# A two-layer decoder trunk on one core: two classes of scales instead of three in the feed-forward output products, part of their exponents on GpSimd, and other places for totals and weight squares

## The chip, the cores and the metric

The kernel runs on one core of a Trainium2 chip. The metric is device time in microseconds (us), the median over several executions. The engines are TensorE (PE in the profile), VectorE (DVE), ScalarE (ACT), GpSimd (POOL) and SyncE (SP), which issues the DMAs.

## The reference, cut to what matters

```python
D_MODEL, SEQ, DEPTH = 1024, 1024, 2
D_FF = 2816                                  # ceil(8 * 1024 / 3 / 256) * 256
...
def swiglu_ffn(x, w_in, w_out):
    gu = jnp.einsum("bsd,df->bsf", x, w_in)
    h = jax.nn.silu(gu[..., :D_FF]) * gu[..., D_FF:]
    return jnp.einsum("bsf,fd->bsd", h, w_out)

def reference(x, ...):
    h = x
    for layer in range(DEPTH):
        hn = rms_norm(h, mix_norm[layer])
        if layer % 2 == 0:
            mixed = rg_lru_block(hn, ...)
        else:
            mixed = stick_breaking_attention(hn, ...)
        h = h + mixed
        h = h + swiglu_ffn(rms_norm(h, ffn_norm[layer]), ffn_w_in[layer], ffn_w_out[layer])
    return rms_norm(h, final_norm)
```

All inputs and the output are f32. The change touches only the feed-forward part, which runs twice, once in each layer, with the same code.

## The kernel before, in words

**Products.** The matrix products of the feed-forward part are computed in a fast form for 2x2 blocks, with 7 products instead of 8. The seven products of a step are numbered k = 0 to 6 in the order in which PE does them. The weights of a product are sums and differences of quarters of the weight matrix: the tiles a, b, c and d (in the profile `wa`, `wb`, `wc`, `wd`). Each factor is held as two f16 tiles, a high part and a low part, so a product takes three matmuls, high by high (L155), high by low (L156) and low by high (L157). The high parts of weights are cut on ACT (L770), the low parts on DVE (L775), which subtracts the high part from the scaled f32 tile. DVE also makes the sums of quarters (L784 to L793).

**Scales.** f16 needs operands of a bounded size. So each tile is multiplied by a power of two before it is cut, and its product by the inverse afterwards. The power comes from a sum of squares: ACT squares a tile and adds up its rows (L753 for the weights of the first product, L1291 for the gated activations U, L1514 for the weights of the second), DVE adds the columns to a `part` of 128x1, PE adds over the partitions by a matmul of one column (L251, into `n_ps`), and a run of small DVE operations shifts exponent bits. A `Measure` does this for the weights of the first product in as many jobs: squares, `total` (L894), and `factors` (the matmul L251 and L244 to L248).

**Steps.** A layer's feed-forward part has steps f = 1 to 21 and then visits v = 0 to 12. Step f forms one of 22 column tiles of gate and up, multiplies silu(gate) by up (L1097 to L1103) into U, and stores operands of the second product, made from pairs of tiles, in DRAM (L1111 to L1127). Visit v multiplies some pairs p0 to p1 of such operands by the output weights and adds the results to the residual h (L1458 to L1464). In layer 0 f1 begins at 342 us, f12 at 547, f20 at 692, f21 at 711, v0 at 732, v2 at 757 and v9 at 884; layer 1 does the same about 1132 us later. Even steps from f4 to f18 also hold the matmuls `i_ps` into 128x256.

**The table of visits** is what the classes of scales cut through:

```python
VISITS = (
    (0, 0, 2), (1, 0, 3), (2, 0, 4), (3, 0, 4), (0, 2, 5), (1, 3, 7), (2, 4, 8),
    (3, 4, 8), (0, 5, 9), (1, 7, 11), (2, 8, 11), (3, 8, 11), (0, 9, 11),
)                                            # (rows d, first pair, end of pairs)
```

Pairs 0 to 3, 4 to 9 and 10 have each a power of their own. A visit over one class has one segment in `Weights`, and each cut of a weight tile is one instruction; a visit over two classes has two segments, and L770 and L775 issue two instructions for each tile, over parts of its columns. Such are v4 and v5 (pairs 3 and 4 in one visit) and v9 to v12 (pairs 9 and 10).

**Order.** PE, ACT, DVE and POOL run in an order that is written by hand: each step calls its pieces product by product, and `plan[kind, x, k]` holds the extra jobs that are put in at product k of step x. `add_up(g)` adds the columns of class g, `scales(g)` does its `n_ps` matmul and the exponents; they stand at (f8: k4, k6), (f20: k4, k6) and (v2: k4, k5). `measure` puts the jobs of each `Measure` into places. `spots` lists the places of the 44 squares L1514 of the output weights in each layer; the DMA that loads such a tile (L1511, 256 KB, on SP) is issued one step earlier at the same k. SP's order is chosen by a scheduler. The seven products share PSUM banks, so some products can begin only after ACT or DVE has read an earlier product out (L1079 and L1083 read products of gate to `G`, L1087 and L1092 those of up to `U`, L1458 those of a visit to `ta`, `tb`, `held` or `G`).

## Time and profile before

| | |
|---|---|
| median of 3 runs | 2097.0 us (2095.85 to 2099.33) |
| profiled execution | 2096.64 us, its span 2094.5 us, granted clock of PE 0.999 |
| PE busy | 2042.5 us, 98% of the span |
| DVE busy | 1853.6 us, 88% |
| ACT busy | 1437.9 us, 69% |
| POOL busy | 104.4 us, 5% |
| DMA | 331.8 MB, 158 GB/s over the span |

The span is one execution seen by the hardware profiler. A row of a timeline has the start, the duration, the engine, the line, the operation, the tiles written and read, and in brackets how long the engine stood idle before it and what released it. Matmuls are pipelined: a row of PE says 0.38 us, and the next begins 0.22 us after it. So PE's busy time runs past the moment at which PE could take the next matmul, and an idle time in brackets is shorter than what was lost by some 0.16 us.

### The profile page before, as it was taken

To read this page: it belongs to the slowest core of one execution; us is meant where nothing else is said; L and a number is where in the kernel's file an instruction comes from. 1 tells how busy PE (TensorE), PEld (TensorE's weight loads), DVE (VectorE), ACT (ScalarE), POOL (GpSimd) and SP (SyncE) were. 2 spreads that over 40 slices of the span, in tenths; PEclk is the share of its full clock that TensorE was granted. 3 is DMA by queue.
4 is the path that set the end of the run, shared out by engine and by line. 5 is a ranking of instruction groups with operands and counts; after the bars stand their busy time and mean duration, and the time that the engine had idled before them with its cause. 6 is when DMAs were issued, how large, how long until landed. Compare 5 with 4: busy or idle time off the path is not lost.

```text
span 2094.5 us, 28835 instructions
## 1 busy us (share of the span) xinstructions
PE 2042.5 (98%) x10058; PEld 1240.3 (59%) x10058; DVE 1853.6 (88%) x2878; ACT 1437.9 (69%) x2369; POOL 104.4 (5%) x114
## 2 busy tenths in 40 slices
PE   8999999999999999989999999999999999999998
PEld 7888885455545444438777777677445555434444
DVE  7887898989999889896999999977899999999887
ACT  6677447777777646566787888744867777765566
POOL 1000010000000000000011111202000000000002
PEclk9999999999999999999999999999999999999999
DMA  7231562644555655134888888972455456764412
GB/s 253 67 94 51 181 206 66 211 156 157 176 186 191 235 192 162 50 111 98 165 176 176 177 177 175 251 230 92 125 168 171 151 186 197 242 225 138 139 41 91
DMA packets 455217, 331.76 MB, mean 158 GB/s; under 512 B 167192, under 2 KB 362912, under 8 KB 455072
## 3 DMA queue, kind: packets, MB, share of 16 engines
q1 hardware_dynamic: 454912, 329.67, 54.6%
q8 instruction: 78, 1.28, 0.3%
q14 instruction: 67, 0.55, 0.1%
q10 hardware_dynamic: 160, 0.27, 0.0%
HBM read 208.74 MB, written 75.50 MB: 136 GB/s over the span
## 4 chain that ended last, share of the span: by engine, by line
PE 71%; DVE 19%; ACT 6%; issue 3%; DMA 1%; SPq 0%; DVEq 0%; ACTq 0%
PE p_ps L157 10%; PE p_ps L155 10%; PE p_ps L156 10%; PE qk_ps L155 4%; PE qk_ps L157 4%; PE qk_ps L156 4%; PE av_ps L2163 3%; PE a_ps L156 3%; PE a_ps L157 3%; PE a_ps L155 3%; PE ob_ps L155 3%; PE ob_ps L156 3%; PE ob_ps L157 3%; DVE v L1366 2%; DVE wa L775 2%
## 5 line engine op out<-in xcount | busy, mean ns | idle before, releaser
L157 PE MATMUL p_ps<-v,wb 128*128 128x512 f16 x524 | 199.5, 381 | 10.5 <-DVE wb L775 10.3
L155 PE MATMUL p_ps<-v,wb 128*128 128x512 f16 x524 | 199.0, 380 | 5.5 <-ACT G L1079 2.4
L157 PE MATMUL p_ps<-v,wc 128*128 128x512 f16 x524 | 198.6, 379 | 2.4 <-DVE wc L775 2.4
L156 PE MATMUL p_ps<-v,wb 128*128 128x512 f16 x524 | 199.3, 380 | 0.0
L155 PE MATMUL p_ps<-v,wc 128*128 128x512 f16 x524 | 198.6, 379 | 0.0
L156 PE MATMUL p_ps<-v,wc 128*128 128x512 f16 x524 | 198.6, 379 | 0.0
L157 PE MATMUL p_ps<-v,wa 128*128 128x512 f16 x396 | 150.1, 379 | 0.0
L156 PE MATMUL p_ps<-v,wa 128*128 128x512 f16 x396 | 150.1, 379 | 0.0
L155 PE MATMUL p_ps<-v,wa 128*128 128x512 f16 x396 | 150.0, 379 | 0.0
L770 ACT ACTIVATE wb<-sb,fac 128x1024 f16<-128x1024 f32 x44 | 50.5, 1148 | 105.4 <-DVE sb L790 105.4
L155 PE MATMUL qk_ps<-rh,whi 128*128 128x512 f32 x264 | 113.0, 428 | 0.0
L2089 ACT ACTIVATE w<-z_ps,rs 128x512 f32<-128x512 f32 (+2 forms) x168 | 96.8, 580 | 16.3 <-PE z_ps L2052 13.1
L155 PE MATMUL p_ps<-v,wd 128*128 128x512 f16 x254 | 96.2, 379 | 11.1 <-ACT G L1458 4.9
L2111 ACT CAST wx<-w 128x512 f16<-128x512 f32 (+1 forms) x140 | 80.1, 572 | 37.4 <-DVE w L2096 19.7
L156 PE MATMUL qk_ps<-rl,whi 128*128 128x512 f32 x264 | 103.5, 392 | 0.0
L157 PE MATMUL qk_ps<-rh,wlo 128*128 128x512 f32 x264 | 103.5, 392 | 0.0
L2096 DVE TENSOR_TENSOR_SCAN w<-w,unit 128x128 f32<-128x128 f32 (+1 forms) x112 | 93.5, 835 | 9.5 <-ACT w L2089 8.3
L157 PEld LDWEIGHTS <-wb 128*128 128x128 f16 x524 | 51.3, 98 | 80.7 <-DVE wb L775 22.6
L1366 DVE SCALAR_TENSOR_TENSOR v<-raw,gx,v 128x512 f16<-128x512 f32 x128 | 91.1, 745 | 7.8 <-ACT v L1365 7.6
L157 PE MATMUL p_ps<-v,wd 128*128 128x512 f16 x254 | 96.3, 379 | 1.5 <-DVE wd L775 1.5
L155 PE MATMUL a_ps<-xh,whi 128*128 128x512 f32 x248 | 97.0, 391 | 0.0
L156 PE MATMUL a_ps<-xl,whi 128*128 128x512 f32 x248 | 96.6, 390 | 0.1
(474 smaller groups left out, 5735.7 us busy)
## 6 DMA issues: line engine op xcount, KB each, us to landing
raw<-in_ffn_w_in SPq DMA_DIRECT2D x80, 512.0 KB, 4.3
raw<-in_ffn_w_out SPq DMA_DIRECT2D x144, 256.0 KB, 3.4
raw<-pd SPq DMA_DIRECT2D x128, 256.0 KB, 3.9
pd<-U SPq DMA_DIRECT2D x90, 256.0 KB, 2.3
raw<-in_attn_w_qkv SPq DMA_DIRECT2D x24, 512.0 KB, 4.3
raw<-in_lru_w_out SPq DMA_DIRECT2D x16, 512.0 KB, 3.5
h<-hd SPq DMA_DIRECT2D x32, 256.0 KB, 5.3
hd<-h SPq DMA_DIRECT2D x32, 256.0 KB, 3.7
```

The lines of the kernel that those rows point to most:

```text
L155: nc.tensor.matmul(ps, lhsT=wh, rhs=mh, start=first, stop=False, **kw)
L156: nc.tensor.matmul(ps, lhsT=wh, rhs=ml, start=False, stop=False, **kw)
L157: nc.tensor.matmul(ps, lhsT=wl, rhs=mh, start=False, stop=last, **kw)
L770: nc.scalar.activation(h, r, AF.Copy, scale=up)
L775: V.scalar_tensor_tensor(l, r, up, h, op0=ALU.mult, op1=ALU.subtract)
L1366: V.scalar_tensor_tensor(lo, raw, power_of(p), hi, op0=ALU.mult, op1=ALU.subtract)
L2089: nc.scalar.activation(F, ps[:, 0:n], AF.Sigmoid, scale=rs[:, j : j + 1])
L2096: nc.vector.tensor_tensor_scan(rev, rev, unit[:, NB - n :][:, ::-1], 0.0, op0=ALU.mult, op1=ALU.add)
L2111: nc.scalar.copy(wx[:, 0:m, 0], F)
L2163: nc.tensor.matmul(ps[:, c0:c1].rearrange("p (j c) -> p j c", c=P), lhsT=VV[q][:, hx, kb], rhs=t, start=first and i == 0, stop=last and i ...
```

## The change

The pairs are put into two classes, 0 to 3 and 4 to 10, instead of three. `segs` and `undo` follow, so v9 to v12 have one segment and v4 and v5 still two. `add_up` and `scales` are called with 0 (class 0), 3 (the output weights) and 1 (class 1) instead of 0, 1 and 2, at (f8: k4, k6), (f20: k4, k6) and (v2: k5, k6). At f20 only the exponent of the output weights is then worked out; that of the second class comes at v2. Some of the small operations (`inverses`, the sums of exponents, two of the `field`s) go to POOL. In `measure`, the squares, total and factors of the `Measure` of f20 move from k0, k1, k1, k2 to k0, k2, k2, k3, and the totals of the pair steps from k6 to k0 of the next step. `spots` is (x, k) for x = 4 to 18 and k = 0, 1, 3 instead of x = 2 to 19 with k = 0, 1 in even and 1, 3, 6 in odd steps; 44 places in both.

```diff
@@ -1267,22 +1267,19 @@
                         nc.sync.dma_start(dst, view[par])
                     return raw
 
-                groups = [int(p >= 4) + int(p >= 10) for p in range(p0, p1)]
-                g, m0 = groups[0], groups.count(groups[0])
-                cols_ = ((3,), (3,))[0] if m0 == m else (4, 5) if g == 0 else (6, 7)
-                segs = [(0, m0, gx[:, cols_[0] : cols_[0] + 1])]
-                if m0 < m:
-                    segs.append((m0, m, gx[:, cols_[1] : cols_[1] + 1]))
+                if p0 < 4 < p1:
+                    segs = [(0, 4 - p0, gx[:, 4:5]), (4 - p0, m, gx[:, 5:6])]
+                else:
+                    segs = [(0, m, gx[:, 3:4])]
                 return Weights(load, m, segs)
 
             def undo(u):
                 _, p0, p1 = VISITS[u]
-                i = 0 if p1 <= 4 else 2 if p0 < 4 else 1 if p1 <= 10 else 3
+                i = 0 if p1 <= 4 else 1 if p0 >= 4 else 2
                 return rx_[:, 4 + i : 5 + i], sums[1][:, i : i + 1]
 
-            power_of = lambda p: gx[:, int(p >= 4) + int(p >= 10) :][:, 0:1]
-            H = rx_.bitcast(I32)
-            G32 = gx.bitcast(I32)
+            power_of = lambda p: gx[:, int(p >= 4) :][:, 0:1]
+            G32, R32 = gx.bitcast(I32), rx_.bitcast(I32)
             tmp = wsq[0][:, 6:8]
             tmpi = tmp.bitcast(I32)
             psq = lambda f: (ymax[:, f : f + 1] if f < 2 * ND else wsq[0][:, f - 2 * ND : f - 2 * ND + 1])
@@ -1290,56 +1287,46 @@
             def square_u(f):
                 nc.scalar.activation(GT[f % 2][:, NB:].bitcast(BF16), UT[f % 3], AF.Square, accum_out=psq(f))
 
-            def add_up(g):
+            def add_up(what):
                 p = part16[0]
                 with nc.allow_low_precision(reason="a bound alone"):
-                    if g == 0:
+                    if what == 0:
                         V.tensor_reduce(p[:, 2:3], ymax[:, 0:8], axis=AX, op=ALU.add)
-                    elif g == 1:
+                    elif what == 3:
+                        V.tensor_reduce(p[:, 2:3], wosq[:, 0 : 2 * NF], axis=AX, op=ALU.add)
+                    else:
                         V.tensor_reduce(tmp[:, 0:1], ymax[:, 8:16], axis=AX, op=ALU.add)
-                        V.tensor_reduce(tmp[:, 1:2], wsq[0][:, 0:4], axis=AX, op=ALU.add)
+                        V.tensor_reduce(tmp[:, 1:2], wsq[0][:, 0:6], axis=AX, op=ALU.add)
                         V.tensor_add(p[:, 2:3], tmp[:, 0:1], tmp[:, 1:2])
-                        V.tensor_reduce(p[:, 3:4], wosq[:, 0 : 2 * NF], axis=AX, op=ALU.add)
-                    else:
-                        V.tensor_add(p[:, 2:3], wsq[0][:, 4:5], wsq[0][:, 5:6])
 
             def field(dst, src, a, b):
-                V.tensor_scalar(dst, src, float(a * EXP), float(b) * EXP, op0=ALU.mult, op1=ALU.add)
-
-            def exponent(at, ps):
-                V.tensor_scalar(tmp[:, 0:1], ps, 1e-30, 1.0, op0=ALU.max, op1=ALU.mult)
-                V.tensor_single_scalar(H[:, at : at + 1], tmpi[:, 0:1], 24, op=ALU.logical_shift_right)
-
-            def both_of(a, at, i):
-                x, y = H[:, a : a + 1], H[:, a + 1 : a + 2]
-                t0, t1 = tmpi[:, 0:1], tmpi[:, 1:2]
-                V.tensor_max(t0, x, y)
-                V.tensor_add(t0, t0, H[:, 3:4])
-                for k, z in enumerate((x, y)):
-                    V.tensor_sub(t1, z, t0)
-                    V.tensor_scalar(t1, t1, -202.0, 203.0, op0=ALU.max, op1=ALU.add)
-                    V.tensor_scalar(G32[:, at + k : at + k + 1], t1, float(EXP), 0.0, op0=ALU.mult, op1=ALU.add)
-                inverse(t0, i)
-
-            def inverse(q, i):
-                field(H[:, 4 + i : 5 + i], q, 1, -25)
-                V.tensor_scalar_mul(sums[1][:, i : i + 1], rx_[:, 4 + i : 5 + i], -1.0)
-
-            def scales(g):
+                eng = nc.vector if dst.shape[-1] == 1 and a < 0 else nc.gpsimd
+                eng.tensor_scalar(dst, src, float(a * EXP), float(b) * EXP, op0=ALU.mult, op1=ALU.add)
+
+            def inverses(q, i, n):
+                field(R32[:, 4 + i : 4 + i + n], q, 1, -25)
+                nc.gpsimd.tensor_scalar_mul(sums[1][:, i : i + n], rx_[:, 4 + i : 4 + i + n], -1.0)
+
+            def scales(what):
                 ps = pp.tile([P, NB], F32, tag="p", name="n_ps")
-                n = 2 if g == 1 else 1
-                over_partitions(ps[:, 0:n], part16[0][:, 2 : 2 + n])
-                exponent(g, ps[:, 0:1])
-                field(G32[:, g : g + 1], H[:, g : g + 1], -1, 203)
-                if g == 1:
-                    exponent(3, ps[:, 1:2])
-                    field(G32[:, 3:4], H[:, 3:4], -1, 203)
-                    for x in range(2):
-                        V.tensor_add(tmpi[:, 0:1], H[:, x : x + 1], H[:, 3:4])
-                        inverse(tmpi[:, 0:1], x)
-                    both_of(0, 4, 2)
-                elif g == 2:
-                    both_of(1, 6, 3)
+                over_partitions(ps[:, 0:1], part16[0][:, 2:3])
+                V.tensor_scalar(tmp[:, 0:1], ps[:, 0:1], 1e-30, 1.0, op0=ALU.max, op1=ALU.mult)
+                V.tensor_single_scalar(tmpi[:, 1:2], tmpi[:, 0:1], 24, op=ALU.logical_shift_right)
+                field(G32[:, what : what + 1], tmpi[:, 1:2], -1, 203)
+                V.tensor_copy(rx_[:, what : what + 1], tmpi[:, 1:2])
+                e0, e1, ew = (rx_[:, x : x + 1] for x in (0, 1, 3))
+                q = sums[0][:, 4:6]
+                if what == 3:
+                    nc.gpsimd.tensor_add(q[:, 0:1], e0, ew)
+                    inverses(q[:, 0:1], 0, 1)
+                elif what == 1:
+                    d = sums[0][:, 6:8]
+                    V.tensor_max(q[:, 1:2], e0, e1)
+                    nc.gpsimd.tensor_add(q[:, 1:2], q[:, 1:2], ew)
+                    nc.gpsimd.tensor_scalar(d, rx_[:, 0:2], q[:, 1:2], -202.0, op0=ALU.subtract, op1=ALU.max)
+                    nc.gpsimd.tensor_scalar(G32[:, 4:6], d, float(EXP), 203.0 * EXP, op0=ALU.mult, op1=ALU.add)
+                    nc.gpsimd.tensor_add(q[:, 0:1], e1, ew)
+                    inverses(q, 1, 2)
 
 
 
@@ -1478,7 +1465,7 @@
                 if (x, k) == (1, 0):
                     m, at = m2, ((1, 0),)
                 elif (x, k) == (NF - 2, 0):
-                    m, at = Measure(nw), ((x, 0), (x, 1), (x, 1), (x, 2))
+                    m, at = Measure(nw), ((x, 0), (x, 2), (x, 2), (x, 3))
                 elif (x, k) == (1, 3):
                     m, at = Measure(ahead), ((1, 3), (1, 4), (1, 5), (2, 0))
                 elif (x, k) == (NF - 4, 4):
@@ -1487,7 +1474,7 @@
                     m, at = Measure(ahead, early[3]), ((2, 0), (2, 1), (2, 4), (2, 5), (2, 6), (3, 2))
                 elif k == 3 and x + 2 in PAIRS and x > 2:
                     m = Measure(ahead, early[x + 1])
-                    at = ((x, 3), (x, 4), (x, 5), (x, 6), (x, 6), (x + 1, 2))
+                    at = ((x, 3), (x, 4), (x, 5), (x, 6), (x + 1, 0), (x + 1, 2))
                 else:
                     m, at = None, ()
                 for i, when in enumerate(at):
@@ -1500,11 +1487,11 @@
             early, squares_of = {}, []
             plan["f", 8, 4] = [lambda: add_up(0)]
             plan["f", 8, 6] = [lambda: scales(0)]
-            plan["f", 20, 4] = [lambda: add_up(1)]
-            plan["f", 20, 6] = [lambda: scales(1)]
-            plan["v", 2, 4] = [lambda: add_up(2)]
-            plan["v", 2, 5] = [lambda: scales(2)]
-            spots = [(x, k) for x in range(2, 20) for k in ((1, 3, 6) if x % 2 else (0, 1))][: 2 * NF]
+            plan["f", 20, 4] = [lambda: add_up(3)]
+            plan["f", 20, 6] = [lambda: scales(3)]
+            plan["v", 2, 5] = [lambda: add_up(1)]
+            plan["v", 2, 6] = [lambda: scales(1)]
+            spots = [(x, k) for x in range(4, 19) for k in (0, 1, 3)][: 2 * NF]
 
             def weigh_out(i):
                 t = loose(v)
```

What this does to the order of the instructions is seen at three places. The first is DVE at the end of f20 and the start of f21 in layer 0. Before, the last seven of 22 small operations of `scales(1)` stand ahead of the gate's product with `ob` (L1097) and the low part of tile b of f21 (L775):

```order
L1319 TENSOR_TENSOR wsq_91<-rx,wsq_91 128x1
L1320 TENSOR_SCALAR wsq_91<-wsq_91 128x1
L1321 TENSOR_SCALAR gx<-wsq_91 128x1
L1307 TENSOR_SCALAR rx<-wsq_91 128x1
L1326 TENSOR_SCALAR sums_94<-rx 128x1
L1097 TENSOR_TENSOR G_2727<-ob,G_2727 128x1024
L775 SCALAR_TENSOR_TENSOR wb<-sb,fac_98,wb 128x1024
```

In the changed program, DVE has there:

```order
L1353 SCALAR_TENSOR_TENSOR rbc_84<-acc_1969,gx,rbc_84 128x512
L1313 TENSOR_SCALAR wsq_91<-n_ps 128x1
L1314 TENSOR_SCALAR wsq_91<-wsq_91 128x1
L1304 TENSOR_SCALAR gx<-wsq_91 128x1
L1316 CAST rx<-wsq_91 128x1
L1097 TENSOR_TENSOR G_2727<-ob,G_2727 128x1024
L775 SCALAR_TENSOR_TENSOR wb<-sb,fac_98,wb 128x1024
```

Here are all the DVE operations of `scales(3)`: four between the low part of an operand of the visits (L1353, which was L1366) and L1097. The names `wsq`, `gx`, `rx` and `sums` are small tiles of exponents and scales.

The second place is ACT from the end of f11 to the middle of f12 in layer 0. `G_2727` and `U_2729` are the gate and up tiles, `wosq` the column of a square of output weights. Before:

```order
L770 ACTIVATE wb<-sb,fac_98 128x1024
L1291 ACTIVATE G_2727,ymax<-U_2731 128x1024
L1092 COPY U_2729<-p_ps 128x512
L1514 ACTIVATE junk,wosq<-raw_1_4262 128x512
L770 ACTIVATE wc<-raw,fac_98 128x1024
L1079 COPY G_2727<-p_ps 128x512
L1514 ACTIVATE junk,wosq<-raw_1_4282 128x512
L1099 ACTIVATE G_2728<-G_2728,fac_97 128x1024
```

After the change (the lines have other numbers: L1291 is L1288, L1514 is L1501):

```order
L770 ACTIVATE wb<-sb,fac_98 128x1024
L1288 ACTIVATE G_2727,ymax<-U_2731 128x1024
L1092 COPY U_2729<-p_ps 128x512
L770 ACTIVATE wc<-raw,fac_98 128x1024
L1079 COPY G_2727<-p_ps 128x512
L1501 ACTIVATE junk,wosq<-raw_1_4277 128x512
L1099 ACTIVATE G_2728<-G_2728,fac_97 128x1024
```

One square, that of f11's k6, has gone from between the reading of a product (L1092) and the high part of tile c (L770); it stood two rows ahead of the reading of f12's first product (L1079). The third place is DVE around v2's products k4 to k6 in layer 0; `part` is what the matmul into `n_ps` reads, `G`, `U` and `tb` are operands of pairs, `s` and `sb` sums of weight quarters, `g` the residual. Before:

```order
L790 TENSOR_TENSOR sb<-raw 128x512
L1304 TENSOR_TENSOR part_95<-wsq_91 128x1
L1124 TENSOR_TENSOR G_2728<-U_2729,tb 128x512
L1464 SCALAR_TENSOR_TENSOR g_2_1_6025<-p_ps,sums_94,g_2_1_6025 128x512
L793 TENSOR_TENSOR s_6676<-sb,raw 128x512
L1310 TENSOR_SCALAR wsq_91<-n_ps 128x1
L1311 TENSOR_SCALAR rx<-wsq_91 128x1
L1307 TENSOR_SCALAR gx<-rx 128x1
L1316 TENSOR_TENSOR wsq_91<-rx 128x1
L1317 ISA wsq_91<-wsq_91,rx 128x2
L1319 TENSOR_TENSOR wsq_91<-rx,wsq_91 128x1
```

After:

```order
L1451 SCALAR_TENSOR_TENSOR g_2_1_6026<-p_ps,sums_94,g_2_1_6026 128x512
L793 TENSOR_TENSOR s_6659<-sb,raw 128x512
L1298 TENSOR_REDUCE wsq_91<-ymax 128x1
L1299 TENSOR_REDUCE wsq_91<-wsq_91 128x1
L1300 TENSOR_TENSOR part_95<-wsq_91 128x1
L1127 TENSOR_TENSOR U_2731<-U_2729,U_2731 128x512
L1451 SCALAR_TENSOR_TENSOR g_6_0_6033<-p_ps,rx,g_6_0_6033 128x512
L1313 TENSOR_SCALAR wsq_91<-n_ps 128x1
L1314 TENSOR_SCALAR wsq_91<-wsq_91 128x1
L1304 TENSOR_SCALAR gx<-wsq_91 128x1
L1316 CAST rx<-wsq_91 128x1
L1324 TENSOR_TENSOR sums_93<-rx 128x1
```

The adding up to `part` is now three operations and stands behind L793 instead of ahead of L1124, and the exponents are four DVE operations (L1313 to L1316) and one for the pair of classes (L1324) instead of thirteen.

## Prediction

> **What bounds the kernel now.** I read the page's busy times and its chain first, then PE's waits, then each wait in the timelines of PE, ACT and DVE.
>
> ```profile
> PE 2042.5 (98%) x10058; PEld 1240.3 (59%) x10058; DVE 1853.6 (88%) x2878; ACT 1437.9 (69%) x2369; POOL 104.4 (5%) x114
> PE 71%; DVE 19%; ACT 6%; issue 3%; DMA 1%; SPq 0%; DVEq 0%; ACTq 0%
> ```
>
> PE sets the time, and the change takes no matmul away. So it can gain only what PE now loses in waits, at the places that it touches. DVE, at 88%, is the engine that makes most of these waits: it carries 19% of the chain. The waits of PE in the whole run (total, times, longest) name the causes:
>
> ```profile
> PE p_ps L157 <- DVE wb L775: 10.3, 11, 2.3
> PE p_ps L155 <- ACT G L1079: 2.4, 9, 0.3
> ```
>
> How much one wait costs is read from PE's timeline at f21 in layer 0:
>
> ```profile
> 716.08 0.38 PE L155 MATMUL p_ps<-v,wb 128*128 128x512 f16 x1
> 716.30 0.38 PE L156 MATMUL p_ps<-v,wb 128*128 128x512 f16 x1
> 718.93 0.39 PE L157 MATMUL p_ps<-v,wb 128*128 128x512 f16 x1 [2.26 <-DVE wb L775]
> ```
>
> Matmuls start 0.22 us apart, though a row says 0.38. The third should have started at 716.52 and started at 718.93: 2.41 us lost where the bracket says 2.26. So each bracket costs 0.15 us more than it says; I add that below.
>
> **The change part by part.**
>
> *The burst of exponents at f20 (`scales(1)`).* DVE's timeline shows the first and the last of its 22 small operations, and what they hold up:
>
> ```profile
> 713.05 0.15 DVE L1310 TENSOR_SCALAR wsq<-n_ps 128x1 f32<-128x1 f32 x1
> 716.40 0.15 DVE L1326 TENSOR_SCALAR sums<-rx 128x1 f32<-128x1 f32 x1
> 716.47 1.22 DVE L1097 TENSOR_TENSOR G<-ob,G 128x1024 f32<-128x1024 f32 x1
> 717.60 1.28 DVE L775 SCALAR_TENSOR_TENSOR wb<-sb,fac,wb 128x1024 f16<-128x1024 f32 x1
> ```
>
> From 713.05 to 716.47 is 3.42 us, 0.155 for each. The change leaves four, 0.62 us, so the gate and `wb` come 2.8 us earlier. `wb`, done at 718.88, would be done at 716.08, which is 0.44 before PE wants it at 716.52. PE comes earlier by what f20 gains (below), but so does DVE, whose wait of 1.23 for the same square ends with it. The whole 2.41 goes, in both layers alike: 4.8. In layer 1 something follows the wait. These are a window right behind it in layer 1, one behind the same wait in layer 0 (length; busy of PE, weight loads, DVE, ACT, POOL; granted clock, DMA share, GB/s), and the wait in layer 1:
>
> ```profile
> 1850.80:1854.20 3.40, 3.40 (x10) 1.17 (x9) 2.46 (x3) 0.00 (x0) 0.00 (x0) 0.51 0.37 108
> 717.90:721.10 3.20, 2.17 (x10) 0.99 (x11) 3.20 (x4) 0.97 (x1) 0.00 (x0) 1.00 0.00 0
> 1850.39 0.39 PE L157 MATMUL p_ps<-v,wb 128*128 128x512 f16 x1 [2.26 <-DVE wb L775]
> ```
>
> At clock 0.51 for 3.4 us PE does 1.7 us less work. Since it begins 0.4 us after the wait, I take the wait for its cause: 1.7 more. [...] The trace is of both kinds, a drop behind the wait in one layer and none in the other.
>
> The moved squares and total of the `Measure` at f20 end a chain of their own:
>
> ```profile
> 699.00 1.06 ACT L753 ACTIVATE junk<-raw 128x1024 bf16<-128x1024 f32 x1 [1.48 <-DMA raw<-in_ffn_w_in]
> 700.18 0.16 DVE L894 TENSOR_REDUCE part<-sums 128x1 bf16<-128x2 f32 x1 [1.23 <-ACT junk L753]
> 700.39 0.16 PE L251 MATMUL n_ps<-part,one 128*128 128x1 bf16 x1 [0.84 <-DVE part L894]
> ```
>
> The square waits for its load, the total for the square, PE for the total: 0.99. Now the square and total stand at k2, the matmul at k3, one product (12 matmuls, 2.6 us) later. That covers the 0.99, twice 2.0; 0.1 in each layer I leave for the matmul itself: 1.8. ACT and DVE no longer stand still behind it, either.
>
> *The squares of output weights (`spots`).* In f2 and f3 squares vanish; at f11's to f17's k6 they go from ahead of the next step's first copy:
>
> ```profile
> 375.53 0.61 ACT L1514 ACTIVATE junk<-raw 128x512 bf16<-128x512 f32 x1
> 376.76 0.38 PE L155 MATMUL p_ps<-v,wb 128*128 128x512 f16 x1 [0.47 <-ACT G L1083]
> 391.50 0.39 PE L157 MATMUL p_ps<-v,wb 128*128 128x512 f16 x1 [0.78 <-DVE wb L775]
> 549.18 0.63 ACT L1514 ACTIVATE junk<-raw 128x512 bf16<-128x512 f32 x1
> 551.47 0.38 PE L155 MATMUL p_ps<-v,wb 128*128 128x512 f16 x1 [0.27 <-ACT G L1079]
> ```
>
> At f2, ACT is late by the squares (0.61 each) just ahead of the copy that PE waits for: two of them, 1.2 us. PE loses 0.62 there and 0.93 at f3, 1.55; ACT being 1.2 earlier can't give more than 1.2, nor less than the 0.62. I take 1.2: 2.4 in both layers. At f12 the square at 549.18 puts off the copy, and PE loses 0.42; the list of waits has nine of these, 0.27 in the mean. Eight are those of f12, f14, f16 and f18 in two layers, 8 x 0.42 = 3.4; the ninth is in f3 and belongs to the term before. The square is longer than the loss (0.63 to 0.42), so nothing is left of it. The same squares now stand at k0, k1 and k3; in an even step the third is a new one. If ACT is as tight at k3 as at k6, each costs 0.42 again (a rival, below).
>
> *The adding up at v2.*
>
> ```profile
> 773.93 0.15 DVE L1304 TENSOR_TENSOR part<-wsq 128x1 bf16<-128x1 f32 x1
> 774.13 0.16 PE L251 MATMUL n_ps<-part,one 128*128 128x1 bf16 x1 [1.57 <-DVE part L1304]
> 775.26 0.68 DVE L793 TENSOR_TENSOR s<-sb,raw 128x512 f32<-128x512 f32 x1
> 775.86 0.15 DVE L1310 TENSOR_SCALAR wsq<-n_ps 128x1 f32<-128x1 f32 x1
> ```
>
> PE loses 1.72: it was ready at 774.13 - 1.72 = 772.41. After the change it comes one product later, at 775.0. DVE does its three operations behind L793, from 775.79 (775.86 less the 0.07 that `part` took) to 776.3. The wait stays, 1.3 instead of 1.7: 0.4 in each layer, 0.8. It could be all 3.4 if DVE comes there earlier, or below nothing if it comes later. DVE's program then has 5 operations where 13 stood (775.86 to 777.95 before), but nothing on PE waits for that up to v3, so I count nothing.
>
> *One segment in v9 to v12.* Two cuts of `wb` on DVE, whole in v8 and in two parts in v9; PE's waits from 880 to 946 us; those from 2012 to 2070 us; and the window of v9 to v12 in layer 0:
>
> ```profile
> 868.16 1.27 DVE L775 SCALAR_TENSOR_TENSOR wb<-sb,gx,wb 128x1024 f16<-128x1024 f32 x1
> 888.20 1.40 DVE L775 SCALAR_TENSOR_TENSOR wb<-sb,gx,wb 128x768 f16<-128x768 f32 x2
> PE p_ps L155 <- ACT held L1458: 2.8, 2, 1.9
> PE p_ps L157 <- DVE wc L775: 1.1, 2, 0.8
> PE p_ps L155 <- ACT ta L1458: 0.9, 2, 0.6
> PE p_ps L157 <- DVE wb L775: 0.5, 1, 0.5
> ```
>
> ```profile
> PE p_ps L155 <- ACT G L1458: 2.6, 2, 2.1
> PE p_ps L155 <- ACT ta L1458: 1.9, 2, 1.0
> PE p_ps L157 <- DVE wc L775: 0.6, 1, 0.6
> 884.00:946.00 62.00, 56.66 (x259) 25.21 (x257) 58.73 (x104) 45.05 (x80) 0.00 (x0) 1.00 0.34 112
> ```
>
> DVE is busy 58.73 of 62 us, so here it sets the pace. A cut in one part saves it 0.13; four tiles, some 0.5 in each visit, four visits, two layers: 4.0. PE's losses there are 5.3 + 7 x 0.15 = 6.3 and 5.1 + 5 x 0.15 = 5.9, so 4.0 fits; the bounds are 0, if ACT holds, and 12.2.
>
> *Scales(0) at f8* gets one DVE operation more (0.155) where no wait stands: nothing; without cover 0.3. *Totals of the pairs* move within DVE's program behind a copy: nothing, since no row of theirs is in the waits; uncovered they cost 0.16 each.
>
> The sum: 4.8 + 1.7 + 1.8 + 2.4 + 3.4 + 0.8 + 4.0 = 18.9. From the execution's own 2096.64 that is 2077.7; the median is 0.4 above it, so **2078**. If every wait went in full it would be 4.8 + 1.7 + 2.0 + 3.1 + 3.4 + 3.4 + 12.2 = 30.6, or 2066. 0.2% is 4.2 us, about what a measurement of this kernel can tell from no change.
>
> **The rivals.**
>
> *POOL holds DVE up.* Nine small operations in each layer go to POOL, whose nearest rows are:
>
> ```profile
> L1909 POOL TENSOR_SCALAR av<-nh 128x1 int32<-128x1 int32 x8 | 6.7, 836 | 0.6
> L1908 POOL TENSOR_SCALAR sv<-nh 128x1 int32<-128x1 int32 x8 | 3.3, 414 | 114.3 <-DVE nh L1905 114.3
> ```
>
> If DVE stood still while POOL works, the three at f21, 1.9 us by the mean of these rows (0.62), less the 0.44 of room, would give back 1.4, and the six at v2, where DVE has no pause, up to 3.8: 5.2 in a layer, 10.4 in all, 2088. Against it: all have one-column operands, and nobody waits for their results before v3. No row shows the two engines side by side. [...] Chance 0.12.
>
> *DVE paces the steps.* Then waits that vanish in f2 to f20 form again later, and only DVE's own saved time counts: 26 operations of 0.155 plus the 2.0 of the visits, 6 in a layer, 12 in all, 2085. Against it stands DVE waiting in turn for ACT, which waits for PE, in f21:
>
> ```profile
> 722.54 0.75 DVE L775 SCALAR_TENSOR_TENSOR wd<-s,fac,wd 128x512 f16<-128x512 f32 x1 [0.74 <-ACT wd L770]
> ```
>
> Chance 0.09. *Squares at k3* cost 0.42 in each of 15 steps and two layers, 12.6: about 2090, chance 0.04.
>
> *Slower: the loads of output weights in SP's queue.*
>
> ```profile
> SPq L1511 <- ACT junk L1514: 132.5, 48, 6.6
> ```
>
> The load L1511 waits in SP's queue for an older square to free its tile, and the loads of the next weights stand behind it. Now three come in each step from f3 on; before it was five in two steps. PE's price for a late weight tile is 0.93 at f3; if each of 15 steps in two layers lost that, it would be 28, against the 18.9 gained: 2106. It decides from the point at which SP's lag passes the lead of the weight loads, two steps of some 18 us each by their starts; waits of up to 6.6 are far from it. Chance 0.06.
>
> *It does not do what it says*: the 22 operations are counted in the order of the changed program as 4, so the burst goes. But several small waits, on POOL, at k3 and in the visits, could fill in to within 4.2 us of the old time, about 2096: 0.07.
>
> **How the numbers follow.** The forecast has 0.62. With POOL 0.12, DVE 0.09 and k3 0.04 faster has 0.87, the same 0.07, slower 0.06. The range goes from 2070, which takes 8 of the 11 us that I left in v2 (2.6) and in the late visits (8.2), to 2091, which holds the first three rivals; what is left out above has 0.13, below some 0.05.
>
> **What would show it.** Right: no bracket at L157 in f21; clock 1.0 at layer 1's f21; no ACT `G` L1079 among PE's waits in f12 to f18; `n_ps` at f20 without bracket, at v2 with one of some 1.2; smaller brackets in v9 to v12. Wrong: DVE rows of f21 or v2 that are longer, or start later, while POOL works; new brackets on L1087's copies at even steps; weights that wait for a DMA. If v0 starts less than 10 us earlier than before in layer 0 and layer 1 together, the steps' gains were given back.

## The result and the profile after

The changed kernel takes 2081.2 us (median of 4 runs, 2080.37 to 2081.99), the kernel before, in the same comparison, 2098.2. The ratio is 0.9917, 95% interval 0.9900 to 0.9935. So the change makes the kernel faster by 17 us; the forecast was 2078, in a range from 2070 to 2091.

The page of the profile after, busy times and chain:

```profile
span 2079.3 us, 28766 instructions
PE 2041.6 (98%) x10058; PEld 1241.7 (60%) x10058; DVE 1840.1 (89%) x2796; ACT 1436.0 (69%) x2339; POOL 110.7 (5%) x132
PE 75%; DVE 16%; ACT 5%; issue 3%; DMA 1%; SPq 0%; DVEq 0%; ACTq 0%
```

PE does the same 10058 matmuls, and its share of the chain has grown at DVE's expense: waits are gone, no work. PE's waits in the whole run:

```profile
PE p_ps L157 <- DVE wb L775: 7.1, 18, 0.7
PE p_ps L155 <- ACT held L1445: 2.6, 2, 1.6
PE n_ps L251 <- DVE part L1300: 2.2, 2, 1.1
PE n_ps L251 <- DVE part L894: 0.9, 1, 0.9
PE p_ps L155 <- ACT G L1079: 0.5, 1, 0.5
```

`wb` fell from 10.3 us to 7.1, but it has 18 waits where it had 11; `G` L1079 fell from 2.4 to 0.5. Both numbers belong together, as will be seen. DVE's timeline at f21 has the first and the last of what is left of the burst, the gate and the cut of `wb`, and PE's the matmul that waited before:

```profile
712.56 0.15 DVE L1313 TENSOR_SCALAR wsq<-n_ps 128x1 f32<-128x1 f32 x1
713.00 0.14 DVE L1316 CAST rx<-wsq 128x1 f32<-128x1 int32 x1
713.06 1.21 DVE L1097 TENSOR_TENSOR G<-ob,G 128x1024 f32<-128x1024 f32 x1
714.19 1.27 DVE L775 SCALAR_TENSOR_TENSOR wb<-sb,fac,wb 128x1024 f16<-128x1024 f32 x1
```

```profile
716.05 0.38 PE L157 MATMUL p_ps<-v,wb 128*128 128x512 f16 x1
```

Four operations stand where 22 did, from 712.56 to 713.06, and the matmul has no bracket.

PE's program is the same in both kernels but for the place of two `n_ps`. So the start of each stretch of matmuls can be set beside that of the same stretch before, and each change of the distance is a gain or a loss at that place. This is the account, in us over both layers (minus is faster):

| place | forecast | measured, layer 0 + layer 1 |
|---|---|---|
| f2 to f4, squares | -2.4 | -1.5 - 1.6 = -3.1 |
| f12 to f18, squares | -3.4 | +0.7 - 0.3 = +0.4 |
| f20, `n_ps` | -1.8 | -0.8 - 0.7 = -1.5 |
| f21, burst (and clock) | -6.5 | -2.5 - 4.2 = -6.7 |
| v2, `n_ps` | -0.8 | -0.5 - 0.5 = -1.0 |
| v9 to v12, one segment | -4.0 | -2.7 - 2.0 = -4.6 |
| loading of inputs, before f1 | 0 | +1.3 |
| sum | -18.9 | -15.2, the difference of the spans |

The last place has nothing to do with the change: in the profiles of this study the work before f1 ends from 0.2 us earlier to 1.9 us later than in that of before. Without it the change gains 16.5.

### The profile page after: what moved, and what is told of

It reads as the page before. It is cut to its first block, busy times and chain, and to the rows that moved or that the text cites. A ratio compares the mean times of both kernels' runs of the same rounds, so it can differ in the third digit from the quotient of the medians.

```text
span 2079.3 us, 28766 instructions
## 1 busy us (share of the span) xinstructions
PE 2041.6 (98%) x10058; PEld 1241.7 (60%) x10058; DVE 1840.1 (89%) x2796; ACT 1436.0 (69%) x2339; POOL 110.7 (5%) x132
## 3 DMA queue, kind: packets, MB, share of 16 engines
q8 instruction: 78, 1.28, 0.3%
## 4 chain that ended last, share of the span: by engine, by line
PE 75%; DVE 16%; ACT 5%; issue 3%; DMA 1%; SPq 0%; DVEq 0%; ACTq 0%
PE p_ps L157 12%; PE p_ps L155 11%; PE p_ps L156 11%; PE qk_ps L155 4%; PE qk_ps L157 4%; PE qk_ps L156 4%; PE av_ps L2150 3%; PE a_ps L156 3%; PE a_ps L157 3%; PE a_ps L155 3%; PE ob_ps L155 3%; PE ob_ps L157 3%; PE ob_ps L156 3%; DVE v L1353 2%; PE z_ps L2038 2%
## 5 line engine op out<-in xcount | busy, mean ns | idle before, releaser
L770 ACT ACTIVATE wb<-sb,fac 128x1024 f16<-128x1024 f32 x44 | 50.5, 1148 | 107.2 <-DVE sb L790 107.2
L1353 DVE SCALAR_TENSOR_TENSOR v<-raw,gx,v 128x512 f16<-128x512 f32 x128 | 91.1, 745 | 6.8 <-ACT v L1352 6.5
```

Source lines behind the costliest of these rows:

```text
L770: nc.scalar.activation(h, r, AF.Copy, scale=up)
L1353: V.scalar_tensor_tensor(lo, raw, power_of(p), hi, op0=ALU.mult, op1=ALU.subtract)
```

## The experiments

Theory: PE's time is the work of its matmuls and its waits, and the terms of the account stand each by itself. Main rival: DVE paces the steps, so what goes at one place comes back at another. All medians below were taken beside runs of the kernel before of 2098.4 to 2099.4; the changed kernel is at 2081.2. Profiles are compared with that of before or after by the starts of PE's stretches, as above. In kernels with added lines, line numbers are some higher.

### One part alone

`spots_only` is the kernel before with one line changed:

```diff
-            spots = [(x, k) for x in range(2, 20) for k in ((1, 3, 6) if x % 2 else (0, 1))][: 2 * NF]
+            spots = [(x, k) for x in range(4, 19) for k in (0, 1, 3)][: 2 * NF]
```

> The kernel before with only the new places of the squares of output weights. Theory (each term of the sum stands by itself): f2 to f4 lose their waits, 3.1 us in both layers, as in the profile after (shifts of 1.5 and 1.6), and the copies of f12 to f18 come early but PE waits for DVE's wb instead, so those steps give nothing: about 3 us less than before, 2095. Rival (the prediction's term): the waits for the copy at f12 to f18 go in full and nothing comes in their place, 3.4 more: 2091 to 2092. Second rival (DVE paces the steps): what f2 to f4 gain is given back by v0, no change.

Measured: 2094.4 us, ratio 0.9983 (0.9974 to 0.9992), 4 us less. f2 to f4 give 1.5 and 1.6, f12 to f18 give 0.0 and 0.3, much as in the profile after; the rival of 3.4 more is refuted. Not expected: f20 gains 0.5 in each layer at `n_ps` from the squares alone. At f21 this profile shows what the clock does behind a wait. PE's wait in each layer and a window right behind it (granted clock third from the end):

```profile
717.78 0.39 PE L157 MATMUL p_ps<-v,wb 128*128 128x512 f16 x1 [2.26 <-DVE wb L775]
1848.41 0.39 PE L157 MATMUL p_ps<-v,wb 128*128 128x512 f16 x1 [2.25 <-DVE wb L775]
```

```profile
718.30:721.50 3.20, 3.20 (x9) 1.08 (x8) 2.35 (x3) 0.00 (x0) 0.00 (x0) 0.50 0.38 113
1848.80:1852.00 3.20, 3.20 (x16) 1.47 (x15) 2.48 (x3) 1.22 (x3) 0.00 (x0) 1.00 0.35 104
```

The same wait, and here the clock is at half in layer 0 and full in layer 1; in the profile of before it was the other way round.

`f20_only` is the kernel before with the `Measure` of f20 moved:

```diff
-                    m, at = Measure(nw), ((x, 0), (x, 1), (x, 1), (x, 2))
+                    m, at = Measure(nw), ((x, 0), (x, 2), (x, 2), (x, 3))
```

> The kernel before with only the squares, total and factors of the Measure at f20 moved. Theory: n_ps at f20 loses its wait, 0.8 in layer 0 and 0.7 in layer 1, and f21 keeps its 2.4 in full, since DVE and PE come earlier alike: 1.5 us less. Rival (the burst eats it): PE comes to f21 earlier and DVE doesn't, and the wait there grows by what f20 gained: no change.

Measured, one execution: 2094.2; since the kernel before spreads over 6 us, it is read by place alone. f20 gains 0.9 and 0.8 at `n_ps`; 0.2 of each comes back by f21, and `wb` of f21 waits 2.26 as before, so DVE and PE come earlier alike. The clock drops behind neither wait here (1.000 granted over the run), which makes this profile 1.6 better in layer 1 than that of before, without any doing of the moved squares.

`scales_only` is the changed kernel with the old lines of `spots`, of the `Measure` of f20 and of the pairs' totals:

```diff
-            spots = [(x, k) for x in range(4, 19) for k in (0, 1, 3)][: 2 * NF]
+            spots = [(x, k) for x in range(2, 20) for k in ((1, 3, 6) if x % 2 else (0, 1))][: 2 * NF]
-                    m, at = Measure(nw), ((x, 0), (x, 2), (x, 2), (x, 3))
+                    m, at = Measure(nw), ((x, 0), (x, 1), (x, 1), (x, 2))
-                    at = ((x, 3), (x, 4), (x, 5), (x, 6), (x + 1, 0), (x + 1, 2))
+                    at = ((x, 3), (x, 4), (x, 5), (x, 6), (x, 6), (x + 1, 2))
```

> The changed kernel with the old places of squares and totals: the two classes, their scales and POOL operations alone. Theory: the wait at f21 goes in both layers with the clock's drop in layer 1 (6.7 us), v2 gives 1.0, the late visits 4.6: 12.3 us less than before, about 2086, and the rest (4.2) belongs to the moved squares and totals. Rival: the gain at f21 needs the earlier DVE that f20's moved total gives, so some 1 us of wait stays at f21 in each layer, and the time is 2088 or more.

Measured: 2084.5, ratio 0.9937 (0.9924 to 0.9949), 13.9 less than before by the medians. By place: f21 -2.5 and -4.2, v2 -0.5 and -0.5, v9 to v12 -2.7 and -2.0: the same as in the full change to a tenth. No wait is left at f21. So the classes and their scales carry some 12.3 of the 16.5, and need nothing of the rest.

### The burst and the clock

`burst_back` is the changed kernel with 18 small operations put back; `burst_long` with 36:

```diff
                 if what == 3:
+                    for _ in range(18):
+                        V.tensor_single_scalar(tmpi[:, 0:1], tmpi[:, 0:1], 1, op=ALU.logical_shift_right)
                     nc.gpsimd.tensor_add(q[:, 0:1], e0, ew)
```

> The changed kernel with 18 more small dependent DVE operations in the exponents of f20, so that 22 stand there again; they change no value that is used. Theory: a wait of PE for wb at f21 of about 2.3 us comes back in both layers, 4.8 us, and the clock drops behind it in layer 1 or in neither: 2086 without the drop, 2087.7 with it. [...] Rival for the wait: something else is late at f21 too, and 18 operations cost less than 2 us in each layer.

Measured: 2088.4, ratio 0.9958 (0.9943 to 0.9973), 7.2 more than the changed kernel. PE's wait at f21 in layer 0 and the windows behind the waits of both layers:

```profile
718.58 0.39 PE L157 MATMUL p_ps<-v,wb 128*128 128x512 f16 x1 [2.57 <-DVE wb L775]
```

```profile
719.20:722.40 3.20, 3.20 (x9) 1.22 (x8) 2.24 (x3) 0.00 (x0) 0.00 (x0) 0.50 0.41 123
1846.50:1849.70 3.20, 3.20 (x17) 1.42 (x16) 2.58 (x3) 1.12 (x3) 0.00 (x0) 1.00 0.31 85
```

The loss comes back at once, 4.2 in layer 0 with a drop and 2.8 in layer 1 without. The burst is the cause at f21.

> The changed kernel with 36 more small DVE operations in the exponents of f20 instead of 18; no value that is used changes. Of the clock: behind losses of 1.3 to 1.8 at a wait no trace showed a drop, behind 2.1 to 2.7 four of fourteen did, behind 5.0 two of two. Theory (the drop depends on how much of a window that runs freely is idle): a loss of some 5.5 at f21 in both layers, with a half clock of some 3 us behind it each time. Rival (only some waits, whatever their length): one or none of the two drops. Time 2081 + 11 + 3.4 = 2095 by the theory.

Measured, one execution: 2098.3; by place f21 costs 8.2 and 7.6. The wait in layer 0 and a window behind the wait of each layer:

```profile
722.81 0.61 PE L157 MATMUL p_ps<-v,wb 128*128 128x512 f16 x1 [5.95 <-DVE wb L775]
```

```profile
722.80:727.10 4.30, 4.29 (x11) 1.55 (x12) 2.88 (x3) 0.00 (x0) 0.00 (x0) 0.50 0.31 91
1854.50:1857.10 2.60, 2.60 (x8) 0.92 (x7) 2.50 (x3) 0.00 (x0) 0.00 (x0) 0.50 0.21 54
```

The loss is 6.1 instead of 5.5, and the clock drops behind both. Over all profiles of this study, PE's losses in the feed-forward parts sort themselves: behind 1.2 to 1.8 us none of 64 was followed by half clock, behind 2.1 to 2.8 four of 16 (the shortest 2.24), behind 5.0 and 6.1 four of four. A drop cost 1.7 at f21 before (4.2 less 2.5 in the account) and 1.5 and 2.1 in `burst_long` (7.6 and 8.2 less the 6.1).

What decides is where a wait falls. Within one profile the stretches of half clock at waits begin whole multiples of 3.413 us apart (718.30 and 2029.02 in `spots_only`, 384 of them; 720.56 and 1850.37 in `burst_long`, 331) and last one or two of them, 3.41 or 6.83 us; in the profile of before the drop at 1850.88 and the half clock at the program's end, from 2093.23, are 242.35 apart, 71 of them. So in these profiles the granted clock changed only at the borders of windows of 3.413 us, and in each profile one such stretch, or the half clock at the program's end, gives all borders. In the profile of before, these are the window that ends at the drop in layer 1, the one behind it, and the two that share the same wait in layer 0:

```profile
1847.47:1850.88 3.41, 1.15 (x7) 0.36 (x5) 3.34 (x7) 1.15 (x1) 0.00 (x0) 1.00 0.00 0
1850.88:1854.29 3.41, 3.41 (x10) 1.21 (x9) 2.38 (x3) 0.00 (x0) 0.00 (x0) 0.50 0.38 111
714.25:717.66 3.41, 2.42 (x12) 0.88 (x9) 3.03 (x17) 0.03 (x1) 0.00 (x0) 1.00 0.39 143
717.66:721.07 3.41, 2.14 (x10) 0.99 (x11) 3.41 (x5) 1.15 (x1) 0.00 (x0) 1.00 0.00 0
```

In layer 1 the whole loss of 2.43 us lies in one window, 0.71 of it; in layer 0 a border cuts the loss of 2.42 into 0.33 of one window and 0.37 of the next. Sorted so, the losses in the feed-forward parts of all 14 profiles leave no exception: where they took 0.66 (2.24 us) or more of a window, half clock followed, and where they took 0.63 (2.13 us) or less, it did not. The loss of 2.7 in layer 1 of `burst_back`, cut into 0.63 and 0.17, dropped nothing; one of 2.24 in `spots_only` that lay in one window did.

### POOL's part

`no_pool` has the same exponents, with all of POOL's operations on DVE:

```diff
-                eng = nc.vector if dst.shape[-1] == 1 and a < 0 else nc.gpsimd
+                eng = V
...
-                    nc.gpsimd.tensor_add(q[:, 0:1], e0, ew)
+                    V.tensor_add(q[:, 0:1], e0, ew)
```

> The changed kernel with the operations of the exponents that it gave to POOL back on DVE: 3 more small ones at f21 and 6 more at v2, 0.15 to 0.19 each. Theory: DVE comes to wb of f21 0.5 later, and there is room for about that, so at most 0.2 is lost there in each layer; at v2 wb comes 1.1 later and PE has room; 2081, the same. Rival (POOL's share is what makes the gain): a wait for wb of 0.5 at f21 and of 1 at v3 in each layer: 2084.

Measured: 2080.4, ratio 0.9919 (0.9904 to 0.9933), the same. No stretch of PE from f18 on moves by over 0.12. The gain is from operations that are no longer there, not from the engine on which the rest run.

How the two engines get on is seen in the profile after, at v2 (POOL, then DVE):

```profile
775.36 1.16 POOL L1325 TENSOR_TENSOR sums<-sums,rx 128x1 f32<-128x1 f32 x1 [61.29 <-DVE sums L1324]
777.88 0.19 POOL L1304 TENSOR_SCALAR rx<-sums 128x2 int32<-128x2 f32 x1
778.16 1.15 POOL L1308 TENSOR_SCALAR sums<-rx 128x2 f32<-128x2 f32 x1
```

```profile
775.19 1.28 DVE L775 SCALAR_TENSOR_TENSOR wb<-sb,gx,wb 128x1024 f16<-128x1024 f32 x1
777.94 1.28 DVE L775 SCALAR_TENSOR_TENSOR wc<-raw,gx,wc 128x1024 f16<-128x1024 f32 x1 [0.34 <-ACT wc L770]
```

These operations of POOL, of one or two columns, take 0.19 to 0.31 when DVE does nothing of the kind, 0.64 beside an addition of 0.69 (L1449), and 1.16 and 1.15 when they meet a cut of a whole tile; each of the two ends within 0.1 of that cut's end (776.47 and 779.22). DVE's cuts keep their 1.28. So here it is POOL that waits, and DVE had begun first. At f21 POOL's three meet the gate L1097 (713.06 to 714.27), which reads `ob` in PSUM and `G` in SBUF, and keep 0.19 to 0.23:

```profile
713.29 0.19 POOL L1320 TENSOR_TENSOR sums<-rx 128x1 f32<-128x1 f32 x1 [386.61 <-PE p_ps L157]
```

To make POOL begin first, `pool_flood` puts 17 operations in front of POOL's own:

```diff
                 q = sums[0][:, 4:6]
+                if what:
+                    nc.gpsimd.tensor_scalar_mul(flood[:, 0:1], rx_[:, what : what + 1], 1.0)
+                    for _ in range(16):
+                        nc.gpsimd.tensor_scalar_mul(flood, flood, 1.0)      # 128x128
```

> The changed kernel with 17 more POOL operations (16 of 128x128) in front of POOL's own at f21 and at v2, in both layers; they compute nothing that is used. Rival A of the prediction (the two engines exclude each other, whichever begins first): POOL often begins first now, so DVE's rows with two SBUF inputs in f21 (wb, wc) and in v2 (wb, wc) grow or start late by up to the length of a POOL row each time, PE waits at f21, and the time goes up by 2 to 10 us, to 2083 to 2091. Theory (POOL gives way): DVE's rows keep 1.28 and no pauses, only POOL's own rows are stretched; 2081, unless the late exponents reach v3 or v4.

Measured: 2094.5, ratio 0.9983 (0.9973 to 0.9992), 13 more. The cuts of f21 on DVE beside the flood, and what ACT and PE wait for in v3 (lines are 2 to 6 higher here):

```profile
714.37 1.33 DVE L777 SCALAR_TENSOR_TENSOR wb<-sb,fac,wb 128x1024 f16<-128x1024 f32 x1
719.83 0.85 DVE L777 SCALAR_TENSOR_TENSOR wd<-s,fac,wd 128x512 f16<-128x512 f32 x1 [1.17 <-ACT wd L772]
```

```profile
789.19 1.12 ACT L772 ACTIVATE wa<-raw,gx 128x512 f16<-128x512 f32 x2 [6.34 <-POOL gx L1333]
```

```profile
791.55 0.38 PE L155 MATMUL p_ps<-v,wd 128*128 128x512 f16 x1 [4.85 <-ACT held L1451]
```

Both sides were wrong in part. DVE now gives way a little: `wb` 1.33 for 1.27, `wd` 0.85 for 0.75, and PE waits for none of it at f21. The whole price, 5.0 and then 1.7 of half clock in each layer (0.54 and 0.51 granted over the 3.4 us from 791.6 and 1921.6), is at v3: ACT needs the exponents of class 1 for v4's `wa`, and they come 11.5 us later (the `gx` of POOL ends at 789.16 instead of 777.64). So the results have some 6.5 us of cover, and past that each us counts. In the rows of v2 above, where DVE began first, POOL's operations lasted until DVE's cut ended (776.52 and 776.47, 779.31 and 779.22). Where POOL began first, no row shows DVE held up by the length of a POOL row: POOL's 0.19 at 777.88 began 0.06 before the cut of `wc`, which kept its 1.28, and in the flood, whose 16 rows run from 713.71 to 726.16, some 0.78 each, `wb` began at 714.37 and took only 0.06 longer than without. Why the two cases differ, no run shows.

### The other terms, and two kernels built on them

`split_back` cuts the tiles of v9 to v12 in two parts again, both with the scale of class 1:

```diff
-                    segs = [(0, m, gx[:, 3:4])]
+                    cut_at = m if p0 < 4 or p1 < 11 else 10 - p0
+                    segs = [(0, cut_at, gx[:, 3:4])]
+                    if cut_at < m:
+                        segs.append((cut_at, m, gx[:, 3:4]))
```

> The changed kernel with the cuts of v9 to v12 in two parts again (at the old border of the third class, both parts with the same scale). Theory (one segment gives the late visits their gain): 2.7 comes back in layer 0 and 2.0 in layer 1, 4.7 in all, and nothing else moves: 2086. Rival (the late visits are better because DVE and ACT come earlier from v2, not because of the segments): the waits of v9 to v12 stay as in the profile after: 2081.

Measured: 2086.3, ratio 0.9938 (0.9923 to 0.9953), 5.1 more than the changed kernel; by place 2.6 and 2.0, all in v9 to v12. The wait of v9, in the changed kernel and with the parts back:

```profile
894.87 0.38 PE L155 MATMUL p_ps<-v,wd 128*128 128x512 f16 x1 [0.99 <-ACT held L1445]
```

```profile
894.57 0.38 PE L155 MATMUL p_ps<-v,wd 128*128 128x512 f16 x1 [1.94 <-ACT held L1448]
```

`sum_early` moves one line of the changed kernel:

```diff
-            plan["v", 2, 5] = [lambda: add_up(1)]
+            plan["v", 2, 4] = [lambda: add_up(1)]
```

> The changed kernel with the adding up of the second class at v2's k4, where it stood before, instead of k5; its exponents stay at k6. Theory (the wait left at v2 is that of the three DVE operations behind L793): part is ready some 2 us before PE comes to n_ps, the wait of 1.10 goes in both layers, and what each costs, 1.25, is gained: 2078.7. Rival (DVE is what PE waits for anyway): the wait comes back within v3 to v5, no change, 2081.

Measured: 2078.8 (2076.7 to 2081.4), ratio 0.9913 (0.9898 to 0.9928). By place 1.3 in each layer, and it does not come back: after the last of DVE's three operations, PE's `n_ps` has no wait:

```profile
769.44 0.16 DVE L1300 TENSOR_TENSOR part<-wsq 128x1 bf16<-128x1 f32 x1
```

```profile
770.26 0.17 PE L251 MATMUL n_ps<-part,one 128*128 128x1 bf16 x1
```

`operand_late` moves the difference of two U halves behind the next gate and cuts:

```diff
                         if gf % 2 == 0:
-                            if k == L - 1 and gf < NF - 2:
-                                operands(gf // 2, 0)
+                            pass
+                        elif k == 1 and gf < NF - 1:
+                            operands(gf // 2, 0)
                         elif 3 <= k <= 5:
```

> The changed kernel with the difference of two U halves (L1113, 0.68 on DVE) behind the gate and the cuts of the next step instead of ahead of them. Theory (in f12 to f18 PE now waits for DVE's wb, and L1113 is one of the operations in front of it): the eight waits of 0.18 to 0.36 go, 0.35 each, 2.8 in all, and f2 and f3 may give some tenths: 2078. Rival (a third engine or ACT is next): the waits stay or turn into ones for ACT, no change.

Measured: 2078.7 (2076.6 to 2082.8), ratio 0.9909 (0.9894 to 0.9924). The changed kernel at f12, DVE's cut and PE's wait, and PE's rows at the same place with `operand_late`:

```profile
550.24 1.27 DVE L775 SCALAR_TENSOR_TENSOR wb<-sb,fac,wb 128x1024 f16<-128x1024 f32 x1
```

```profile
551.58 0.39 PE L157 MATMUL p_ps<-v,wb 128*128 128x512 f16 x1 [0.18 <-DVE wb L775]
```

```profile
551.47 0.38 PE L156 MATMUL p_ps<-v,wb 128*128 128x512 f16 x1
551.69 0.38 PE L157 MATMUL p_ps<-v,wb 128*128 128x512 f16 x1
```

f12 to f18 gain 1.7 and 1.4, so it was DVE's work in front of `wb` that replaced the squares. f2 and f3 come out even.

> The changed kernel with the sum of the second class at v2's k4 and with L1113 behind the next step's gate and cuts. Theory (the two gains, 2.6 and 2.8 by their traces, are of different places and add): 2076. Rival (DVE's time gained in the steps is lost by v2): no better than one alone, 2078.7.

Measured: 2077.5 (2076.2 to 2079.0), ratio 0.9899 (0.9882 to 0.9915). The two gains are there in full (v2 1.3 and 1.3, f12 to f18 1.7 and 1.4), but f3 has a new wait, which costs 1.7 and 1.5, a little more than f2 and f3 gain:

```profile
390.04 0.59 ACT L1079 COPY G<-p_ps 128x512 f32<-128x512 f32 x1 [1.50 <-DMA pd<-G]
```

ACT may not write into `G` until an operand in it has been stored. That store is issued at 385.42 and lands at 389.94, 4.5 us later; in the changed kernel it is issued at 386.13 and lands at 389.64, 3.5 us later. So it is not the issue that is late but the store that takes longer; why is not shown.

`wb_first` has `sum_early`'s line and the cut of `wb` ahead of the gate:

```diff
-                elif gf is not None and s_:
+                elif gf is not None and s_ and kind == "v":
                     gate(gf, 0)
                 if not w.ready:
                     w.b_lo()
                     if kind == "f":
                         w.c_hi()
+                if not odd and s_ and kind == "f":
+                    gate(gf, 0)
```

> The changed kernel with the sum of the second class at v2's k4 and with DVE cutting wb's low part ahead of the gate's first product in the steps, instead of behind it. Theory (PE waits in f2, f3 and f12 to f18 for wb, which stands behind a gate of 1.2): wb comes 1.2 earlier, the waits of 0.6 in f2 and f3 (0.75 each, four) and those of f12 to f18 (0.35 each, eight) go, 5.8 less than with the early sum alone (2078.8): 2073. Rival (the gate is what ends last): silu on ACT comes 1.2 later, DVE then waits for ACT, and the same or more is lost for wc, wd or G: 2078 or above.

Measured: 2077.4 (2074.7 to 2077.9), ratio 0.9893 (0.9878 to 0.9908): some 1.4 of the 5.8 that were expected over `sum_early` by the medians. By place f12 to f18 give 1.5 and 1.3, but in f2 and f3 the waits mostly change hands: 0.8 goes at `wb` in each, and 0.4 to 0.6 comes back at a copy that waits for ACT. In layer 0:

```profile
377.88 0.38 PE L155 MATMUL p_ps<-v,wb 128*128 128x512 f16 x1 [0.46 <-ACT G L1083]
391.34 0.38 PE L155 MATMUL p_ps<-v,wb 128*128 128x512 f16 x1 [0.36 <-ACT G L1079]
```

There the rival held. Both kernels beat the changed one by some 4 us, and the intervals of their ratios and of its own overlap a little; that they gain at these places is shown by the traces, how much in the median is not settled better than that.

## Why the prediction was right, point by point

- **PE bound, gain in its waits.** Right: the account above is complete with PE's waits, and its sum is the difference of the spans. Of the 18.9 of the forecast 15.2 came in these two profiles: f12 to f18 fell short by 3.8 and the loading of inputs took 1.3, and that the other places gave 1.4 more than their sum was luck in their sizes.
- **The burst at f20 and f21.** Right in cause and size, 6.7 for 6.5: `burst_back` brings it back. There was room, too: DVE starts the cut of `wb` at 714.19 and is done at 715.46, and PE wants it at 716.05, 0.6 later, where 0.44 was worked out.
- **The clock.** The 1.7 was right for the one profile of before, and right in its cause, the wait. But it is not layer 1's: it hangs on where the wait falls between two borders. By an estimate from the figures above, a loss of 2.42 us has 2.2 us or more in one window in some 0.4 of all positions, (3.41 - 2.42 + 2 x 0.22) / 3.41, so the two waits of f21 cost some 1.4 us of half clock in the mean of many runs. The kernel before spreads over 6 us and the changed one over 1.6, and the spread goes with the clock: of 36 executions of the kernel before, three with a mean granted clock of 1.000 have spans of 2091.6 to 2093.8 us, eleven with 0.999 have 2094.2 to 2096.9, and 22 with 0.998 or 0.997 have 2095.0 to 2099.2.
- **f20's `n_ps`.** Right, 1.5 for 1.8. The moved squares of output weights alone do much of it, so the two causes overlap.
- **Squares of output weights.** f2 to f4 gave 3.1 for 2.4; 0.3 of it in each layer came at f4, which the sum did not have. For f12 to f18 the step that failed is "The square is longer than the loss (0.63 to 0.42), so nothing is left of it". It asked whether the copy would still be late and not what was late next. DVE's cut and PE's need of it, in the kernel before at f12:

```profile
550.48 1.27 DVE L775 SCALAR_TENSOR_TENSOR wb<-sb,fac,wb 128x1024 f16<-128x1024 f32 x1
```

```profile
551.90 0.38 PE L157 MATMUL p_ps<-v,wb 128*128 128x512 f16 x1
```

`wb` ended at 551.75, 0.15 before PE came to it, and only since PE had lost 0.42 just ahead. With the copy in time PE waits for `wb` and gives 0.35 of the 0.42 back. `operand_late` shows that it is DVE's work in front of it. So the rival that DVE paces the steps held in these eight, and nowhere else. In layer 0 one more wait, 0.48 at f17, comes behind a store of `G` that had not landed; the profiles of the other kernels have it with 0.27 to 0.88 or not at all, and its cause stays open.
- **v2.** Right, 1.0 for 0.8; that the wait would be 1.3 instead of 1.7 came to 1.27.
- **v9 to v12.** Right, 4.6 for 4.0, shown by `split_back`.
- **The sign for the steps.** v0 was to start over 10 us earlier in both layers together. Counted from f1 of each layer, it starts 4.2 and 6.7 earlier, 10.9.
- **The rivals.** POOL holding up DVE: where the two met at v2, it was POOL that waited (1.16 and 1.15 us, DVE's cuts kept 1.28), and its results have 6.5 us of cover. Squares at k3: no wait at those copies. Loads of output weights in SP's queue: its waits went from 132.5 us in 48 to 111.7 in 42, and no wait of PE in the steps and visits is for a weight's DMA:

```profile
SPq L1498 <- ACT junk L1501: 111.7, 42, 6.0
```

## What to carry to other kernels

A wait that is taken away is worth the distance to what comes next, not its length: read the ends of all operands of the waiting instruction, and of the next one or two, before counting a gain. A run of tiny operations on a dense engine delayed what stood behind it by its whole length (22 of them 3.4 us on VectorE), and here it mattered that they were fewer and not on which engine they ran. A wait on TensorE can cost twice: in layer 1 of the profile of before 2.43 us were lost, and 1.7 more at half clock, with 0.71 of one window lost; the 2.42 of layer 0 fell across a border and cost no more. So a single profile of such a kernel has or has not the drop by chance.

## What was not expected of the hardware

- In the 14 profiles, half clock for a window of 3.41 us or two after one of which TensorE's wait took 0.66 or more (2.24 us), and never where it took 0.63 or less. So a loss of 2.24 us dropped the clock and one of 2.7 did not.
- In the profile after, the GpSimd operations of the exponents, on one or two columns, took 0.19 to 0.31 us alone and beside the gate L1097, 0.64 beside L1449, and 1.16 and 1.15 beside the cuts of `wb` and `wc`, until those ended; VectorE's cuts there kept their 1.28, and its rows at f21 grew by 0.1 at most beside the flood (0.85 for 0.75).
